# Rotating a batch of images: loads of 16 rows to a partition, with two images alternating on neighbouring partitions

## The chip, the cores and the metric

The kernel runs on one core of a Trainium2 chip. The metric is the device time of one execution in microseconds. The time before is 124.72 us, the median of 4 runs (124.68 to 124.79).

## The reference

```python
batch, c, h, w = 32, 3, 256, 256
x = np.random.randn(batch, c, h, w).astype(np.float32)

def reference(x):
    return np.rot90(x, k=-1, axes=(-2, -1)).astype(np.float32)
```

There are 96 images of 256 x 256 fp32 values, 256 KiB each, 25.17 MB in all. Each is turned by a quarter clockwise: `out[i, j] = x[255 - j, i]`. So a row of the output is a column of the input read from bottom to top. No value is changed; everything is movement.

## The kernel before

An image is cut into 32 strips of 8 rows. One strip goes to one partition (8 rows of 1 KiB, contiguous in DRAM, 8 KiB), so the 32 partitions of a quadrant hold one image and the 128 partitions hold four. This is a slab of 1 MiB, and there are 24 slabs.

For each slab, the loop at L42 does the following.

- L44: one load of 1 MiB into `t_in`, issued on the queue of SyncE (SP).
- L47 and L48 make two views. In `src` the order within a partition is column-in-group `c` (8), row `r` (8), column group `g` (32). In `dst` it is the same, but `g` now stands on the place where the partition index of the input comes out, and row and strip run backwards.
- L51: two transposes on VectorE, each for four values of `c`, 1024 elements a partition. The instruction takes the elements of a partition 32 at a time and transposes each 32 x 32 block within a quadrant: element `g` of partition `p` becomes element `p` of partition `g`. After that partition `g` holds the 8 output rows that belong to the input columns 8g to 8g+7, 8 KiB, contiguous in the output.
- L53: one store of 1 MiB from `t_out`, issued on the queue of ScalarE (ACT).

Both tiles have 12 buffers of 8 KiB a partition. A framework orders the instructions and puts in the waits: a transpose waits for its load, a store for the transposes, a load for a free buffer. It counts landings on eight semaphores, which all loads and stores use in turn; a transfer that gets a semaphore again is issued only when the transfer that had it before has landed. No order is written out by hand. PE isn't used, and GpSimd writes four constants that nothing reads.

Of the kernel before, what the change touches and what calls it, by code (L numbers as in the profile page):

```python
# [1 line left out]

# [4 lines left out]


@with_exitstack  # L10
def kernel(
    ctx: ExitStack,
    tc: tile.TileContext,
    x: bass.AP,
    out: bass.AP,
):

    nc = tc.nc
    fp32 = mybir.dt.float32

    B, C, H, W = x.shape
    P = nc.NUM_PARTITIONS
    R = 8  # L30
    G = H // R
    n_slabs = B * C * G // P
    PARTS = 2
    CP = R // PARTS

    ld_v = x.rearrange("b c h w -> (b c h) w").rearrange("(n p r) w -> n p (r w)", p=P, r=R)
    st_v = out.rearrange("b c h w -> (b c h) w").rearrange("(n p c) w -> n p (c w)", p=P, c=R)

    in_pool = ctx.enter_context(tc.tile_pool(name="in_pool", bufs=12))
    out_pool = ctx.enter_context(tc.tile_pool(name="out_pool", bufs=12))  # L40

    for n in range(n_slabs):  # L42
        t_in = in_pool.tile([P, R * W], fp32, tag="t_in")
        nc.sync.dma_start(out=t_in, in_=ld_v[n])  # L44

        t_out = out_pool.tile([P, R * W], fp32, tag="t_out")
        src = t_in.rearrange("p (r g c) -> p c r g", r=R, c=R)  # L47
        dst = t_out.rearrange("p (c g r) -> p c r g", c=R, r=R)[:, :, ::-1, ::-1]  # L48
        for k in range(PARTS):
            cs = slice(k * CP, (k + 1) * CP)  # L50
            nc.vector.transpose(out=dst[:, cs], in_=src[:, cs])  # L51

        nc.scalar.dma_start(out=st_v[n], in_=t_out)  # L53


# [1 line left out]
_INS = ['x']  # L57
_OUTS = [((32, 3, 256, 256), 'float32')]


# [23 lines left out]
```

## Time and profile before

| | us |
|---|---|
| median of 4 runs | 124.72 |
| the profiled execution, its own time | 124.71 |
| span of its instructions | 122.9 |
| VectorE busy, 48 transposes | 94.6 |
| one transpose, median | 2.040 |
| first load issued, landed | 0.73, 5.53 |
| first transpose begins | 5.55 |
| first store issued | 9.56 |
| last load issued, landed | 92.11, 111.67 |
| last store issued, landed | 115.81, 122.12 |

The time of an execution is a little longer than the span, which goes from the first instruction to the last. The profile splits the span into 40 slices and tells for each what share of it an engine was busy and how many GB/s the 16 DMA engines moved. A queue is named by a number: q1 carries the loads, q10 the stores. A DMA's packet is a piece that one DMA engine moves; every DMA also sends one small packet from each engine, which counts on the semaphore. "SPq" and "ACTq" are the sequencers that issue the DMAs. A row of a group of instructions gives the busy time and the mean of one in ns, and then how long the engine stood idle before them and what ended this.

### The profile page before, as it was taken

To read this page: it belongs to the slowest core of one execution; us is meant where nothing else is said; L and a number is where in the kernel's file an instruction comes from. 1 tells how busy PE (TensorE), PEld (TensorE's weight loads), DVE (VectorE), ACT (ScalarE), POOL (GpSimd) and SP (SyncE) were. 2 spreads that over 40 slices of the span, in tenths; PEclk is the share of its full clock that TensorE was granted. 3 is DMA by queue.
4 is the path that set the end of the run, shared out by engine and by line. 5 is a ranking of instruction groups with operands and counts; after the bars stand their busy time and mean duration, and the time that the engine had idled before them with its cause. 6 is when DMAs were issued, how large, how long until landed. Compare 5 with 4: busy or idle time off the path is not lost.

```text
span 122.9 us, 186 instructions
## 1 busy us (share of the span) xinstructions
DVE 94.6 (77%) x48; POOL 0.2 (0%) x4
## 2 busy tenths in 40 slices
DVE  0199999999797697886977969779769788696600
POOL 0000000000000000000000000000000000000000
DMA  3999999999999999999999999999999999999993
GB/s 96 424 427 381 363 427 427 427 429 429 427 427 427 427 427 427 429 429 427 427 429 427 427 427 427 429 429 429 427 429 429 427 427 429 427 427 427 427 427 160
DMA packets 6913, 50.34 MB, mean 410 GB/s; under 512 B 768, under 2 KB 768, under 8 KB 768
## 3 DMA queue, kind: packets, MB, share of 16 engines
q1 hardware_dynamic: 3456, 25.17, 49.4%
q10 hardware_dynamic: 3456, 25.17, 48.5%
q14 instruction: 1, 0.01, 0.0%
HBM read 25.17 MB, written 25.17 MB: 409 GB/s over the span
## 4 chain that ended last, share of the span: by engine, by line
DMA 79%; DVE 11%; DVEq 2%; SPq 1%; issue 0%
DMA t_in<-in_x_dram 41%; DMA out_dram<-t_out 38%; DVE t_out L51 11%; DVEq L79 2%; SPq L44 1%
## 5 line engine op out<-in xcount | busy, mean ns | idle before, releaser
L51 DVE STREAM_TRANSPOSE t_out<-t_in 128x1024 f32<-128x1024 f32 x48 | 94.6, 2054 | 21.2 <-DMA t_in<-in_x_dram 10.0
L68 POOL MEMSET const-uint8-127<- 128x1 uint8 x1 | 0.1, 102 | 0.0
L68 POOL MEMSET const-bfloat16-1.0<- 128x1 bf16 x1 | 0.1, 101 | 0.0
L68 POOL MEMSET const-float32-0.0<- 128x1 f32 x1 | 0.1, 98 | 0.2 <-issue 0.2
L68 POOL MEMSET const-float32-1.0<- 128x1 f32 x1 | 0.1, 98 | 0.0
## 6 DMA issues: line engine op xcount, KB each, us to landing
t_in<-in_x_dram SPq DMA_DIRECT2D x24, 1024.0 KB, 19.6
out_dram<-t_out ACTq DMA_DIRECT2D x24, 1024.0 KB, 16.3
```

Source lines behind the costliest of these rows:

```text
L44: nc.sync.dma_start(out=t_in, in_=ld_v[n])
L51: nc.vector.transpose(out=dst[:, cs], in_=src[:, cs])
L68: nc = _bacc.Bacc("TRN2", target_bir_lowering=False, num_devices=1)
L79: with _tile.TileContext(nc) as tc:
```

## The change

A partition now takes 16 rows (16 KiB) of an image, so an image takes 16 partitions, and a quadrant of 32 partitions holds two images. They alternate: partition `2k + i` of a quadrant has strip `k` of image `i`. A slab is 8 images, 2 MiB, and there are 12 slabs. The load is still one DMA over 128 partitions; its source is a view of three dims, 64 strips x 2 groups of images x 4096 elements, and its rows are 16 KiB long.

A transpose now handles one of the 8 values of `c`, 512 elements a partition (16 rows by 32 column groups), and its 32 outputs to a partition are 16 strips of each of two images. They go alternately to the two halves of `t_out`, which lie 8 KiB apart, one half for each image. So there are 8 transposes to a slab, 96 in all. The output keeps its strips of 8 rows: each half is stored by a DMA of its own of 1 MiB with 8 KiB to a partition, two to a slab and 24 in all. Both tiles have 6 buffers of 16 KiB a partition, the same space as before.

```diff
-    R = 8
-    G = H // R
-    n_slabs = B * C * G // P
-    PARTS = 2
-    CP = R // PARTS
+    RI, RO = 16, 8
+    K, G = H // RI, H // RO
+    I = 2
+    Q = P // (K * I)
+    n_slabs = B * C // (Q * I)
 
-    ld_v = x.rearrange("b c h w -> (b c h) w").rearrange("(n p r) w -> n p (r w)", p=P, r=R)
-    st_v = out.rearrange("b c h w -> (b c h) w").rearrange("(n p c) w -> n p (c w)", p=P, c=R)
+    ld_v = x.rearrange("b c h w -> (b c h) w").rearrange(
+        "(n i m r) w -> n i m (r w)", i=I, m=Q * K, r=RI)
+    st_v = out.rearrange("b c h w -> (b c h) w").rearrange(
+        "(n i p c) w -> n i p (c w)", i=I, p=P, c=RO)
 
-    in_pool = ctx.enter_context(tc.tile_pool(name="in_pool", bufs=12))
-    out_pool = ctx.enter_context(tc.tile_pool(name="out_pool", bufs=12))
+    in_pool = ctx.enter_context(tc.tile_pool(name="in_pool", bufs=6))
+    out_pool = ctx.enter_context(tc.tile_pool(name="out_pool", bufs=6))
 
     for n in range(n_slabs):
-        t_in = in_pool.tile([P, R * W], fp32, tag="t_in")
-        nc.sync.dma_start(out=t_in, in_=ld_v[n])
+        t_in = in_pool.tile([P, RI * W], fp32, tag="t_in")
+        nc.sync.dma_start(out=t_in, in_=ld_v[n].transpose([1, 0, 2]))
 
-        t_out = out_pool.tile([P, R * W], fp32, tag="t_out")
-        src = t_in.rearrange("p (r g c) -> p c r g", r=R, c=R)
-        dst = t_out.rearrange("p (c g r) -> p c r g", c=R, r=R)[:, :, ::-1, ::-1]
-        for k in range(PARTS):
-            cs = slice(k * CP, (k + 1) * CP)
-            nc.vector.transpose(out=dst[:, cs], in_=src[:, cs])
+        t_out = out_pool.tile([P, I, RO * W], fp32, tag="t_out")
+        src = t_in.rearrange("p (r g c) -> p c r g", r=RI, c=RO)
+        dst = t_out.rearrange("p i (c k r) -> p c r k i", c=RO, r=RI)[:, :, ::-1, ::-1, :]
+        for c in range(RO):
+            nc.vector.transpose(out=dst[:, c], in_=src[:, c])
 
-        nc.scalar.dma_start(out=st_v[n], in_=t_out)
+        for i in range(I):
+            nc.scalar.dma_start(out=st_v[n, i], in_=t_out[:, i])
```

## The prediction

> **What bounds the kernel now.** I read the overview of the page first (engines, slices, queues), then the chain of waits, then the queue's own waits, then the timeline of VectorE, and last windows of 1 us at the start, at the dip that the slices show, and at the end.
>
> ```profile
> span 122.9 us, 186 instructions
> DVE 94.6 (77%) x48; POOL 0.2 (0%) x4
> GB/s 96 424 427 381 363 427 427 427 429 429 427 427 427 427 427 427 429 429 427 427 429 427 427 427 427 429 429 429 427 429 429 427 427 429 427 427 427 427 427 160
> q1 hardware_dynamic: 3456, 25.17, 49.4%
> q10 hardware_dynamic: 3456, 25.17, 48.5%
> DMA 79%; DVE 11%; DVEq 2%; SPq 1%; issue 0%
> ...
> t_in<-in_x_dram SPq DMA_DIRECT2D x24, 1024.0 KB, 19.6
> out_dram<-t_out ACTq DMA_DIRECT2D x24, 1024.0 KB, 16.3
> ```
>
> The bytes per slice are flat at 427 to 429 GB/s from the second slice to the last but one, with one dip (381, 363). The two queues together are busy for 97.9% of 16 engines' span, VectorE for 77%, and 79% of the chain that ended last is transfers. The DMA engines are the bound. What is hard to move is 25.17 MB in and 25.17 MB out: 50.33 MB / 0.4275 MB/us = 117.7 us.
>
> ```profile
> 1.00:2.00 1.00, 0.00 (x0) 0.00 (x0) 1.00 0.45 66
> 2.00:3.00 1.00, 0.00 (x0) 0.00 (x0) 1.00 0.61 221
> 3.00:4.00 1.00, 0.00 (x0) 0.00 (x0) 1.00 0.95 401
> ...
> 11.00:12.00 1.00, 1.00 (x2) 0.00 (x0) 1.00 0.96 303
> 12.00:13.00 1.00, 1.00 (x1) 0.00 (x0) 1.00 1.04 328
> 13.00:14.00 1.00, 1.00 (x2) 0.00 (x0) 1.00 0.95 320
> ...
> 120.00:121.00 1.00, 0.00 (x0) 0.00 (x0) 1.00 0.89 377
> 121.00:122.00 1.00, 0.00 (x0) 0.00 (x0) 1.00 0.16 66
> ```
>
> The last two columns are the DMA share and the GB/s. The rest of the span is here. Start: 0 to 4 us moved 0+66+221+401 = 688 KB where 1710 were possible, a loss of 2.4 us. Dip, just as the first stores join the loads: 951 KB in 3 us where 1282 were possible, 0.8 us. End: 443 KB in the last 2.9 us where 1253 were possible, 1.9 us (landing of the last store and the closing waits). 117.7 + 2.4 + 0.8 + 1.9 = 122.8 against the span of 122.9. The profiled execution took 124.71 us, 1.8 us of it outside the span, and the median is 124.72, so a change of the span is taken as a change of the median.
>
> ```profile
> SPq L44 <- DMA t_in<-in_x_dram: 82.0, 19, 4.7
> DVE t_out L51 <- DMA t_in<-in_x_dram: 10.0, 6, 5.5
> 5.55 26.86 DVE L51 STREAM_TRANSPOSE t_out<-t_in 128x1024 f32<-128x1024 f32 x14 [5.55 <-DMA t_in<-in_x_dram]
> 33.20 3.99 DVE L51 STREAM_TRANSPOSE t_out<-t_in 128x1024 f32<-128x1024 f32 x2 [0.78 <-DMA t_in<-in_x_dram]
> ```
>
> The landing records show eight semaphores in rotation over all 48 transfers; the sixth and every later load waits until the load that had its semaphore before has landed, so about four loads (4 MB) are in flight, and the DMA engines never lack one. VectorE runs without a gap up to 32 us and then has 4.0 us of work for each 4.9 us (2 x 1.05 MB / 0.4275), in which one slab goes in and one out. It waits; nothing waits for it but the first store and the last.
>
> **The change, part by part.**
>
> (1) Load packets. 24 loads of 128 packets of 8 KB plus 16 completion packets (24 x 144 = 3456, the q1 line) become 12 loads of 128 packets of 16 KB plus 16: 1728. Stores stay at 24 with 3456. Gone are 1536 data packets and 192 completions, that is 96 and 12 on each engine. A completion packet takes 9 ns in the packet records, so 12 x 9 ns = 0.1 us. What a data packet costs beside its bytes the trace doesn't show: an 8 KB packet has 309 ns in the records, and at 427.5 GB/s one leaves each engine every 306.6 ns, so packets overlap a little. From below it is nothing (a gain of 0.1 us with the completions); from above the 9 ns of a packet of 4 bytes, 96 x 9 = 0.9 us (1.0 us in all). I take a third, 3 ns: 0.3 + 0.1 = 0.4 us gained, nearer to nothing, since records that overlap speak for small gaps.
>
> The Trainium skill (DMA: Bandwidth & Descriptors, "Why small descriptors are slow") gives about 3 cycles of overhead a packet; at the 850 MHz it names for the fabric that is an estimate of 3.5 ns, by which the gain would be 96 x 3.5 + 108 = 0.44 us. [...]
>
> (2) The loads' source now has three dims (64 x 2 x 4096), two images 1 MB apart alternating on neighbouring partitions, the destination still 128 partitions. No row has such a source. If the same 16 engines share it evenly, it costs nothing; I take that, as 64 and 128 both divide by 16, and whole rows of 16 KB are contiguous. If the engines got in each other's way, loads would go at less than 427 GB/s; that is under the rivals.
>
> (3) VectorE: 48 transposes of 1024 elements become 96 of 512, the same 49,152 elements a partition. Back to back, 14 take 26.86 us: (26.86 - 2.04) / 13 = 1.91 us from start to start, 2.04 us for one. Half of 1.91 is 0.955, the lower end if nothing is fixed. If the 0.13 us by which one is longer than the pitch is a fixed cost of each, it is (1.91 + 0.13) / 2 = 1.02. What is not in any row is the new write: neighbouring elements alternate between two places 8 KB apart, with 64 B steps instead of 32 B. From below, a write spread over two places might even be quicker, which would be worth nothing under the transfers; from above, an instruction doesn't get shorter at all (1.91). I take 1.0 us, by the nearest row: 96 us in all, for a slab of 2 MB 8.0 us against 9.8 us of transfers. It is hidden by the DMA's 117.7 us. The cover ends where first landing + 96 pitches + the end fill the span: 8.0 + 96p + 7.7 = 122.9, so p = 1.12 us (7.7 = two stores 4.9, issue, first packet and landing 2.0, closing 0.8).
>
> For that the Trainium skill (VectorE: DVE Perf Modes, "The TRN2 errata") speaks against the change: a fixed cost for every instruction, about 58 cycles, hence few large instructions. By its figure, an estimate, VectorE gets 48 x 60 ns = 2.9 us more work, all of it under the transfers.
>
> (4) Start. The first load of 2 MB lands 2.45 us later (1.05 MB / 0.4275): 5.5 becomes 8.0. Eight transposes make the first store issue at about 16.1 instead of 9.56. This costs nothing while loads fill the DMA: in 13 us they move 5.6 MB, and the eight semaphores let four or five loads of 2.1 MB go before one must wait for a store. The dip of 0.8 us when stores join moves to about 18 us; I leave its size, between 0 and twice as much (packets twice as long), as unknown: 124.7 minus or plus 0.8.
>
> (5) End. Before, the last load's packets end at 111.0 and the stores' at 121.65: 10.6 us of stores, 4.55 MB, are still to go, which is the lead that the loads got before the first store. The first store moves by 6.5 us, so the lead grows by 6.5 x 0.4275 = 2.8 to 7.35 MB. The last slab needs 0.7 (landing) + 8.1 (transposes) + about 2 (issue to first packet) = 10.8 us after the last load packet; the other 7.35 - 2.1 = 5.25 MB of stores keep the DMA busy for 12.3 us. So 1.5 us of cover is left, no bubble. The very last stores are 1 MB as before: end 1.9 us unchanged.
>
> (6) Queues. A slab now issues one load and two stores, so the rotation of eight makes a load wait for a store of the slab four or five before it, not for a load. With five, loads may lead by about 9 MB, with four by 6.9 MB; the lead is 7.35, so at worst it is cut by 0.45 MB, and 0.4 of the 1.5 us of cover at the end is left: nothing. Behind a waiting load on SP stand only loads; behind a store on ACT only stores. Buffers: six of 2 MB hold the same 12 MB.
>
> Sum: 122.9 - 0.4 = 122.5 us of span, and 124.72 - 0.4 = **124.3 us**.
>
> **The rivals.**
>
> (A) Forecast: DMA-bound as now, packets 0.1 to 1.0 us cheaper: 123.7 to 124.6, likeliest 124.3. Chance 0.55: 0.38 faster, 0.17 within the noise.
>
> (B) The rate doesn't depend on packet length at all, or the longer dip eats the gain. For it: 427 GB/s whether loads run alone or beside stores. Against it: half the completions do go. 124.5 to 124.9, about 124.7. Chance 0.15 (0.01 faster, 0.11 same, 0.03 slower).
>
> (C) VectorE becomes the bound, through the scattered write of alternating 8 KB steps. For it: even now an element takes 1.86 ns, and nothing says that the write isn't what sets this. Against: all accesses are strided already. It decides from a pitch of 1.12 us, 12% over my value; at 1.15 the span is 8.0 + 110.4 + 7.7 = 126.1 (127.9 us), at 1.25 it is 135.7 (137.5 us). Chance 0.15, all slower.
>
> (D) A bubble: loads with two images share the engines unevenly, or the semaphore wait on a store holds a load back, or transposes eat the cover of 1.5 us at the end. For it: slabs twice as coarse make every wait twice as long. Against: 4 to 5 MB of stores stand ready. 1 to 3 us: 125.5 to 127.5. Chance 0.15 (0.01 same, 0.14 slower).
>
> **How the numbers follow.** A measurement of this kernel (124.68 to 124.79) tells about 0.2%, 0.25 us, from no change. Faster 0.38 + 0.01 = 0.39; same 0.17 + 0.11 + 0.01 = 0.29; slower 0.03 + 0.15 + 0.14 = 0.32. The time is that of (A), 124.3, whose own range is 123.7 to 124.6. To leave out no more than 2 in 10 the range takes in (B), (D) and the foot of (C): 123.7 to 128.
>
> **What would show it.** Right: load queue 1728 packets; GB/s flat at 427 to 431 from 4 us on; transposes of 512 near 1.0 us apart, with gaps of over 1 us after each eight once the first third is done; first store near 16 us; last load packets near 105 us and no slice under 420 after that until the last. Wrong: transposes over 1.12 us apart and running without a gap to the end (C); slices under 400 in the middle or between the last load and the last store (D); the sum of the start, dip and end losses more than 5.5 us (B).

## The result and the profile after

The changed kernel takes 124.75 us in the median of 53 runs, before 124.72 us in 73. The ratio is 1.0033 with a 95% interval of 1.0020 to 1.0045, so it is 0.2 to 0.5% slower, although the medians are nearly equal. The reason is in the spread: before lies between 124.58 and 125.19; the changed kernel has 30 of its 53 runs from 124.43 to 124.81 (the lower group), three at 125.0, and 20 from 125.43 to 126.65 (the upper group). The profiled execution is one of the three (125.0 us); no run of the lower group left a profile.

First the overview of the changed kernel.

```profile
span 123.2 us, 199 instructions
DVE 96.6 (78%) x96; POOL 0.2 (0%) x4
GB/s 122 388 415 431 442 442 306 404 420 439 450 407 434 420 439 442 407 439 436 402 426 449 418 426 457 396 426 434 447 423 428 428 418 428 428 428 426 426 434 117
q1 hardware_dynamic: 1728, 25.17, 48.7%
q10 hardware_dynamic: 3456, 25.17, 48.3%
DMA 54%; DVE 32%; DVEq 1%; issue 1%; SPq 0%
t_in<-in_x_dram SPq DMA_DIRECT2D x12, 2048.0 KB, 12.9
out_dram<-t_out ACTq DMA_DIRECT2D x24, 1024.0 KB, 19.2
```

The load queue has its 1728 packets, and the two queues need 97.0% of 16 engines' span (97.9% before): the packets did get cheaper. The bytes per slice still stand near 427 throughout. (They scatter more, since a 16 KB packet is counted in the slice in which it starts.) A load of twice the size lands 12.9 us after its issue in the median, where the smaller one took 19.6. That is the first sign of something not foreseen: loads now hurry ahead of stores.

The waits of the queue, the waits of VectorE, and its timeline:

```profile
SPq L46 <- DMA out_dram<-t_out: 74.0, 7, 19.9
SPq L46 <- DMA t_in<-in_x_dram: 5.3, 1, 5.3
DVE t_out L52 <- DMA t_in<-in_x_dram: 12.5, 3, 8.6
8.60 64.27 DVE L52 STREAM_TRANSPOSE t_out<-t_in 128x512 f32<-128x512 f32 x64 [8.60 <-DMA t_in<-in_x_dram]
```

64 transposes take 64.27 us, a pitch of 1.0 us as forecast. The gaps after each eight that the forecast expected from the first third on aren't there: until 73 us slabs come in as fast as VectorE works. And seven of the twelve loads wait for the landing of a store, 74 us together; before, all waited for loads.

The packet records give a second reading. Take the time that has passed less (bytes moved / 428.3 GB/s): this is the mean loss of the 16 engines in us at that time. Beside it: when no load packet was on any engine for over 2 us after 28 us ("dry"); how long packets ran beyond their usual 309 or 611 ns after 28 us, summed over the engines ("stretched", in engine-us); and the time between the first and the last of the 16 landings of the last store. The last column is that execution's own time. These are sums over packet and landing records, one execution of each kernel.

| kernel | loss at 4 | at 18 | at 28 | at 120 | loads dry, us | stretched | last landings | time |
|---|---|---|---|---|---|---|---|---|
| before | 2.50 | 3.41 | 3.43 | 3.64 | none | 0.7 | 0.94 | 124.71 |
| changed | 2.77 | 2.81 | 3.63 | 3.64 | 40.9-45.4, 60.3-64.7, 80.0-84.5 | 2.0 | 1.23 | 125.00 |
| changed, again | 3.07 | 2.98 | 3.48 | 3.71 | 40.3-45.2, 61.6-66.2, 81.3-85.8 | 5.7 | 2.15 | 125.88 |
| contiguous | 2.85 | 2.77 | 3.12 | 3.63 | 39.9-43.9, 60.6-64.8, 81.0-84.2 | 10.1 | 2.46 | 125.92 |
| one store | 2.97 | 2.90 | 3.55 | 3.44 | none | 1.4 | 1.07 | 124.55 |
| load in halves | 3.01 | 3.08 | 3.72 | 3.95 | none | 0.6 | 0.90 | 125.17 |
| small start | 2.60 | 3.12 | 3.13 | 2.96 | none | 0.8 | 1.03 | 124.24 |

Read the first two rows from the left. The start costs 0.3 us more, and the first stores 0.8 as before, only later. From 28 to 120 us before loses 0.21 us more and the changed kernel none: that is most of the gain of the long packets. At 120 us both stand at 3.64. The third row has nearly the same mean at 120 and yet ends 0.9 us later, because its engines don't end together. The time is set by the slowest of 16 engines.

### The profile page after: what moved, and what is told of

Its sections match the earlier page's. It is cut to its first block, busy times and chain, and to the rows that moved or that the text cites. A ratio compares the mean times of both kernels' runs of the same rounds, so it can differ in the third digit from the quotient of the medians.

```text
span 123.2 us, 199 instructions
## 1 busy us (share of the span) xinstructions
DVE 96.6 (78%) x96; POOL 0.2 (0%) x4
## 3 DMA queue, kind: packets, MB, share of 16 engines
q1 hardware_dynamic: 1728, 25.17, 48.7%
## 4 chain that ended last, share of the span: by engine, by line
DMA 54%; DVE 32%; DVEq 1%; issue 1%; SPq 0%
DVE t_out L52 32%; DMA out_dram<-t_out 31%; DMA t_in<-in_x_dram 23%; DVEq L81 1%; DVEq L52 0%; SPq L46 0%
## 5 line engine op out<-in xcount | busy, mean ns | idle before, releaser
L52 DVE STREAM_TRANSPOSE t_out<-t_in 128x512 f32<-128x512 f32 x96 | 96.6, 1094 | 12.5 <-DMA t_in<-in_x_dram 12.5
## 6 DMA issues: line engine op xcount, KB each, us to landing
t_in<-in_x_dram SPq DMA_DIRECT2D x12, 2048.0 KB, 12.9
```

What stands on the lines that cost most here:

```text
L52: nc.vector.transpose(out=dst[:, c], in_=src[:, c])
```

## The experiments

**The changed kernel again.** No edit.

> The changed kernel again, for a second profile. Its 53 times so far fall in two groups, 30 from 124.4 to 124.8 and 20 from 125.4 to 126.7 us. Theory S (the source of two images 1 MB apart disturbs some executions), theory Q (a load that waits for a store's landing is sometimes late), theory K (slabs of 2 MB, whatever the packets) and theory L (packets of 16 KB share the engines badly with packets of 8 KB) all expect the two groups again, about 4 of 10 runs over 125.3. A profile that falls in the upper group should lose its 1 to 2 us in one place: at the start or in the dip (L, S), spread over the middle (S), or in a bubble beside a late load (Q).

Measured: 125.86 us median of 6 (124.77 to 126.75, five of them over 125.6), ratio 1.0072 (1.0044 to 1.0100). The profile fell in the upper group. Its end in windows of 1 us (the last columns are the DMA share and GB/s); before moved its last bytes at 66 GB/s from 121 to 122 and none after that:

```profile
120.00:121.00 1.00, 0.00 (x0) 0.00 (x0) 1.00 0.91 385
121.00:122.00 1.00, 0.00 (x0) 0.00 (x0) 1.00 0.18 74
122.00:123.00 1.00, 0.00 (x0) 0.00 (x0) 1.00 0.04 16
```

A share of 0.04 from 122 to 123 is less than one engine of 16 at work, while 15 are done. So the loss isn't at the start, in the dip, or spread over all engines: a straggler is 1.5 us behind the median landing (121.56, 123.11). Stretched packets stand at 45 to 48, 51, 59, 68, 86 to 92 and 97 to 100 us, most of them soon after the load queue had run dry and started again.

Do they make the straggler? The records don't name the engine, but nearly every packet begins 3 or 4 ns before another ends, so they can be joined into 16 chains (all but some 2 to 4%). The chain that ends last, at 122.78 us, has 1.55 engine-us of stretched packets, four of its seven from 45 to 48 us; the other 15 end by 121.88 with at most 0.93 each. In the contiguous kernel of the next run the four chains that end last (121.99 to 122.82) have 1.3 to 1.9 each, the other twelve at most 0.7. So in both traces the engines that end last are those with the most stretched packets.

**A contiguous source.**

```diff
-        "(n i m r) w -> n i m (r w)", i=I, m=Q * K, r=RI)
+        "(n m r) w -> n m (r w)", m=P, r=RI)
-        nc.sync.dma_start(out=t_in, in_=ld_v[n].transpose([1, 0, 2]))
+        nc.sync.dma_start(out=t_in, in_=ld_v[n])
```

> The load's source is one contiguous run of 2 MB, 16 KB to a partition, images not alternating; transposes and stores unchanged, so the images come out in scrambled places, with the same bytes and the same work. Theory S: the upper group is gone, all runs 124.4 to 124.8. Theories Q, K and L: as the changed kernel, about 4 of 10 runs over 125.3.

Measured: 126.25 us median of 4 (125.92 to 126.40), ratio 1.0125 (1.0111 to 1.0140). The alternating images aren't the cause: without them all four runs are in the upper group. Theory S falls. Why it is always there with this source and in four of ten runs with the other wasn't found.

**One store for each slab.**

```diff
-        for i in range(I):
-            nc.scalar.dma_start(out=st_v[n, i], in_=t_out[:, i])
+        nc.scalar.dma_start(out=st_v[n].transpose([1, 0, 2]), in_=t_out)
```

> One store of 2 MB for each slab in place of two of 1 MB, so that loads and stores alternate in the rotation of eight semaphores and a load waits for a load again. Theory Q: the upper group is gone, all runs 124.4 to 124.8. Theories S, K and L: about 4 of 10 runs still over 125.3.

Measured: 124.48 us median of 11 (124.41 to 124.55), ratio 0.9979 (0.9971 to 0.9988). The upper group is gone, and the kernel is a little faster than before. Its waits of the queue and its issue rows:

```profile
SPq L46 <- DMA t_in<-in_x_dram: 47.0, 7, 9.3
SPq L46 <- DVE t_out L52: 2.1, 3, 1.3
...
t_in<-in_x_dram SPq DMA_DIRECT2D x12, 2048.0 KB, 29.5
out_dram<-t_out ACTq DMA_DIRECT2D x12, 2048.0 KB, 24.5
```

Loads wait for loads again, several are in flight (29.5 us to landing), and none runs dry.

**Slabs of 2 MB with 8 KB packets.** The layout of before, two of its slabs in one load.

```diff
-    ld_v = x...rearrange("(n p r) w -> n p (r w)", p=P, r=R)
+    ld_v = x...rearrange("(n i p r) w -> n i p (r w)", i=2, p=P, r=R)
-        nc.sync.dma_start(out=t_in, in_=ld_v[n])
+        nc.sync.dma_start(out=t_in, in_=ld_v[n].transpose([1, 0, 2]))
```

> The layout and the transposes of before (8 rows, 8 KB packets, 1024 elements), but slabs of 2 MB: one load of 256 packets of 8 KB, two stores, six buffers. Theory K or Q: two groups, about 4 of 10 runs over 125.3. Theories S and L: one group, and the packet term of the forecast makes it no faster than before: 124.6 to 125.0.

Measured: 124.79 us median of 11 (124.47 to 124.88), ratio 1.0001 (0.9992 to 1.0009). Its loads wait for stores too:

```profile
SPq L45 <- DMA out_dram<-t_out: 71.4, 7, 13.6
```

Yet it has one group, no dry spell over 0.2 us, and its last landings lie within 0.47 us. So neither the slab of 2 MB nor the wait for a store is enough (K falls, Q in its plain form too); the long packet is left as what else it takes, and the next two runs test it. The packet records tell what it does. From 47 to 58 us the changed kernel moves 286 GB/s in and 145 out, 1.97 to 1; before, from 30 to 60, it is 213.6 to 213.8. That fits engines that take a packet from each queue in turn, where a load packet is now twice as long; in the chains of the changed kernel nine of ten neighbours from 47 to 58 us belong to different queues. This is theory R of the next runs.

**Contiguous source, load packets of 8 KB.** `max_dma_last_dim=8192` added to the load of the contiguous kernel.

> As the kernel with the contiguous source (images scrambled, same bytes), but its loads cut into packets of 8 KB, 256 to a load; slabs, transposes, stores and the rotation of semaphores unchanged. Theory R: packets of 16 KB and 8 KB take turns on each engine, so loads get two thirds, outrun the semaphores that they wait for, the load queue runs dry about three times for 4 us, and each restart stretches packets on a few engines, which then end 1 to 2 us after the others. With 8 KB on both sides the shares are equal, the queue doesn't run dry for more than 0.3 us, the last store's 16 landings lie within 1.0 us, and the time is 124.5 to 124.9. Rival theory P (the rotation with store waits or the contiguous source costs by itself, whatever the packets): 125.9 to 126.4 as before it.

Measured: 124.86 us median of 11 (124.77 to 125.02), ratio 1.0011 (1.0002 to 1.0020). Packet length alone takes 126.25 to 124.86: shares 1.06 to 1, no dry spell, last landings within 0.95 us. The waits for stores are still there; in the contiguous kernel with 16 KB packets and in this one they are

```profile
SPq L46 <- DMA out_dram<-t_out: 76.8, 7, 19.6
SPq L46 <- DMA out_dram<-t_out: 76.0, 7, 17.9
```

As R said, against P.

**Contiguous source, one store for each slab.** The contiguous source and the single store together, 16 KB packets.

> The contiguous source with 16 KB packets (images scrambled), but one store of 2 MB for each slab, so that no load waits for a store. Theory R: loads still get two thirds, but the load queue never runs dry in the middle; 124.2 to 124.6. Rival theory H (reading 16 KB rows of one contiguous 2 MB run is slow or uneven by itself): 125.9 to 126.4, with landings of the last store over 2 us apart.

Measured: 124.21 us median of 6 (124.15 to 124.55), ratio 0.9967 (0.9955 to 0.9978). One store in place of two, and the rotation that changes with it, takes 126.25 to 124.21. As R said, against H.

**One store, three load buffers.** `in_pool` from 6 to 3 buffers in the kernel with one store.

> One store of 2 MB for each slab as in the run that stayed at 124.4 to 124.6, and three buffers for the loads in place of six, so that a load now waits for the transposes of the third slab before it; no load waits for a store. Theory R (a dry load queue and its restart cost, whatever it waited for): the queue runs dry at most slabs, the landings of the last store spread to over 1.5 us, 125.3 to 127. Rival theory Q (it is the wait on a store's landing that costs): 124.4 to 124.6 still.

Measured: 125.86 us median of 4 (125.75 to 125.99), ratio 1.0093 (1.0079 to 1.0107). The time is as R expected, but not for R's reason. Its windows around the first store (DVE busy, POOL, clock, DMA share, GB/s):

```profile
17.00:18.00 1.00, 1.00 (x2) 0.00 (x0) 1.00 0.56 229
18.00:19.00 1.00, 1.00 (x2) 0.00 (x0) 1.00 1.15 377
19.00:20.00 1.00, 1.00 (x2) 0.00 (x0) 1.00 0.98 205
20.00:21.00 1.00, 1.00 (x2) 0.00 (x0) 1.00 1.01 336
21.00:22.00 1.00, 1.00 (x2) 0.00 (x0) 1.00 1.13 344
22.00:23.00 1.00, 1.00 (x2) 0.00 (x0) 1.00 0.81 295
```

With three buffers the first three loads end at 18 us just as the first store comes, and this dip costs 2.2 us of all engines instead of 0.8. After that the load queue is dry eight times for 0.1 to 0.9 us, and none of these costs anything; the last landings lie within 0.94 us. This run can't speak for R.

**A small start.** One store for each slab, the first 8 images as two slabs of the kernel before, and five large buffers on each side in place of six.

```diff
+    for n in range(I):
+        s_in = small_in.tile([P, RO * W], fp32, tag="s_in")
+        nc.sync.dma_start(out=s_in, in_=ld_s[n])
...
+        nc.scalar.dma_start(out=st_v[0, n], in_=s_out)
-    for n in range(n_slabs):
+    for n in range(1, n_slabs):
```

> One store for each slab of 2 MB, and the first 8 images as two slabs of the kernel before (1 MB, 8 KB packets, two transposes of 1024). Theory R with the start as a separate loss (the first packets of the three-dim load begin at 2.1 us where those of before begin at 1.7): loss at 4 us falls from about 2.9 to 2.5 us, no dry queue, 124.0 to 124.3. If the start loss has nothing to do with the form of the first load: 124.4 to 124.6.

> The kernel with a small start again, for the interval: 124.0 to 124.3 by theory R, with no load dry for over 0.5 us.

Measured: 124.18 us median of 5 (124.08 to 124.29), ratio 0.9957 (0.9943 to 0.9970), and in a second set of runs 124.14 of 5 (124.10 to 124.18), ratio 0.9957 (0.9945 to 0.9968). The loss at 4 us is 2.60 where the kernel with 2 MB from the start has 2.97. The form of the first load isn't all that counts: every kernel that begins with 2 MB loses 2.76 to 3.07, the contiguous and the 8 KB ones too. Nor is its size: the last kernel below begins with 1 MB from the source of three dims and loses 3.01. Only the load of before, plain and of 1 MB, loses 2.50 to 2.60. This version beats both kernels, by 0.5 us.

**Loads run dry for want of buffers.** One store; four buffers for the first four slabs, two for the other eight.

> One store for each slab of 2 MB (no load waits for a store); the buffers of the loads are divided, four for the first four slabs and two for the other eight, so that from the seventh slab on a load waits for the transposes of the slab two before it. The start is as with six buffers. Loads should run dry once for about 11 us (from about 40) and then about five times for 2 to 3 us, while stores keep the DMA engines busy. Theory R (a load queue that was dry for several us and starts again stretches packets on some engines): stretched packets 2 to 6 us after each such restart, 1 or more engine-us each, the landings of the last store over 1.5 us apart in most executions, 125 to 127. Rival theory Q (only waits on a store's landing on all 16 engines do this): no stretched packets after 28 us, 124.4 to 124.7.

Measured: 128.16 us median of 6 (127.45 to 130.50), ratio 1.0269 (1.0242 to 1.0295). In windows of 2 us:

```profile
90.00:92.00 2.00, 2.00 (x3) 0.00 (x0) 1.00 1.15 430
92.00:94.00 2.00, 2.00 (x3) 0.00 (x0) 1.00 0.92 307
94.00:96.00 2.00, 2.00 (x3) 0.00 (x0) 1.00 0.88 324
...
116.00:118.00 2.00, 2.00 (x4) 0.00 (x0) 1.00 0.61 254
118.00:120.00 2.00, 1.11 (x2) 0.00 (x0) 1.00 0.00 0
```

The load queue was dry at 39 to 53, 68 to 72 and 89 to 92 us. The first restart stretched nothing, the second 0.7 engine-us, the third 15 (91 to 96 us: the DMA share stays near 0.9 and the bytes fall). That one had waited for transposes, not for a landing, so a wait for a landing isn't needed. Another 2.5 us went into a bubble near 119 in which the last slab was late and no queue had work, so the time can't be laid to restarts alone, and the landings, all delayed by the bubble, don't show the spread expected.

**Two dry spells, nothing else.** One store, five load buffers and one that slabs 4, 7 and 10 share.

> One store for each slab of 2 MB as in the run that stayed at 124.4 to 124.6; five buffers for the loads and one shared by slabs 4, 7 and 10, so that load 7 waits for the transposes of slab 4 (until about 49) and load 10 for those of slab 7 (until about 73). The load queue should be dry twice for 3 to 9 us and stores should fill the DMA engines all the while; no load waits for a store. Theory R (restart after several dry us stretches packets, not each time): stretched packets of 0 to 15 engine-us within 6 us of each restart, the landings of the last store over 1.2 us apart, times spread from 124.5 to 126.5 with a median over 124.8. If a restart costs nothing: 124.4 to 124.6 and no stretched packets after 28 us beyond the single one of 0.5 us.

Measured: 124.51 us median of 11 (124.38 to 124.69, and one of 125.27), ratio 0.9991 (0.9980 to 1.0003). The load queue was dry from 46.8 to 52.8 us and for 1.2 us at 76. No packet was stretched behind either, the single one of 0.5 us at 65 us aside. A dry spell of 6 us can cost nothing: R in this form was wrong.

**One dry spell with 8 KB packets.** Before, with 11 load buffers and one that slabs 11 and 12 share.

> The kernel before, with 11 buffers for the loads and one shared by slabs 11 and 12, so that load 12 waits for the transposes of slab 11. The load queue is dry once, for about 6 us from about 60, and the stores that are ready (some 3 MB) fill the DMA engines. Packets are 8 KB on both sides. Theory R without a part for packet length: stretched packets of 0 to 15 engine-us behind the restart, 124.7 to 126, runs spread over more than 0.5 us. If long packets are needed for it: 124.6 to 124.9 like before, no stretched packets after 28 us.

Measured: 124.68 us median of 11 (124.56 to 124.91), ratio 1.0002 (0.9993 to 1.0011). The dry spell didn't come about (none over 0.1 us): inconclusive.

**Three stores for each slab.** The second store of the changed kernel cut into 7 rows and 1.

> The changed kernel with the second store of each slab cut into 7 rows and 1 row of a partition, three stores a slab: four transfers a slab, so that the rotation of eight lets a load wait for the load two before it and for no store. Loads keep 16 KB packets. If the rotation is the cause (the load queue runs dry for 4 us because a load waits for a store's landing): no dry spell over 2 us after 28 us, the last landings within 1.2 us, all runs within 0.5 us of each other, at 124.6 to 125.2 (1536 more store packets cost up to 0.5 us). If stores in several DMAs beside long load packets are the cause whatever the rotation: two groups again, with runs 1 to 2 us over the lowest.

Measured: 125.35 us median of 5 (125.20 to 125.42), ratio 1.0053 (1.0040 to 1.0065). One group, so several stores don't make two by themselves, as far as five runs tell (with four in ten in the upper group, five would miss it about once in 13). It is 0.15 us above the range expected. Against the expectation there is a dry spell (31.4 to 38.0): two loads still waited for stores. Stretched packets follow from 38 to 45 (2.5 engine-us), and after 85 us, with stores alone, short packets cost 0.4 us. Landings lie 1.12 us apart.

**The changed kernel, each load in two halves.** Two DMAs of 8 rows to a partition.

> The changed kernel with each load cut into two DMAs of 8 rows a partition, so 8 KB packets and 1 MB each; two stores a slab as before. Four transfers a slab. If long packets and the dry queue are the cause: shares of loads and stores equal, no dry spell over 0.5 us after 28 us, all runs 124.5 to 125.0. If the alternating source or the scattered transposes are the cause: runs up to 126 again.

Measured: 125.15 us median of 5 (125.10 to 125.34), ratio 1.0040 (1.0027 to 1.0054). One group, shares 0.99 to 1, nothing dry: the alternating source and the scattered transposes by themselves don't make runs of 126, again as far as five runs tell. The edit undoes both sides at once, the long packets and the waits for stores (17 of its 18 waits are for loads), so it doesn't part them. The level is 0.15 over what I expected. Against the kernel with one store its loss grows by 0.23 from 28 to 120 us where the other's falls by 0.11.

## Why the prediction was wrong

By its own steps:

(1) **Packets: right.** The records have 309 ns for 8 KB with the next packet 306 ns after it, and 611 for 16 KB with the next after 607: 2 x 306 - 607 = 5 ns for each packet saved, where I took 3. 96 x 5 + 12 x 9 ns = 0.6 us. The kernel with one store loses 0.34 us less from 28 to 120 than the one with 8 KB halves. The Trainium skill (DMA: Bandwidth & Descriptors, "Why small descriptors are slow") puts it at about 3 cycles, by my estimate 3.5 ns; the measured 5 ns agree in size.

(2) **The source of three dims: nearly right.** Pure loads run at 428 GB/s and more (611 ns each), evenly enough. With one store the contiguous source took 124.21 where this one took 124.48 (ratios 0.9967 and 0.9979, whose intervals overlap), so up to 0.3 us may be the price of three dims; the first packet comes at 2.10 us instead of 1.72.

(3) **VectorE: right.** A pitch of 1.0 us, and rival (C) is out: it idles 12.5 us waiting for loads, 8.6 of them before the first.

(4) **Start: wrong by 0.3 to 0.5 us.** I moved the first landing to 8.0 us (measured: 8.6) and called the rest free. The loss at 4 us is 2.5 to 2.6 with the first load of before and 2.8 to 3.1 with all others, whether they have 2 MB in the plain form (2.85, 3.04) or 1 MB in three dims (3.01). What makes it wasn't taken apart. The dip kept its size (0.8), as assumed.

(5) **End: right, with luck.** There was no bubble. But the last load packet ended at 99.4 us, not near 105, with 9.3 MB of stores still to go instead of 7.35, because loads had more than half of the engines, which the step didn't foresee. Stores filled the engines until 121.

(6) **Queues: the step that failed.** It says of the lead: "at worst it is cut by 0.45 MB", and of the cost: "nothing". It reckoned with equal shares and some 2 us from issue to first packet. Measured: loads get two bytes for each one of stores, so a load of 2 MB is through in 7.3 us where slabs take 9.8; and a load issued onto engines that are busy with stores has its first packet 4 us later (issued at 41.30, 60.84, 80.70; first packets at 45.35, 64.71, 84.54). The lead of the loads was 7.46 MB when the first store's packets began (20.7 us), as forecast (7.35); but it didn't stay there, it grew to 9.2 MB by 41 us. That is the bound of about 9 MB that the step itself gives for five slabs. (In the kernel with 2 MB slabs and 8 KB packets the lead never exceeds 6.8 MB.) So the lead ran up against the landing that a load waits for, and the queue was dry for 4.5 us three times. That stores keep the DMA busy meanwhile was right; that it costs nothing was not. The Trainium skill (DMA: Bandwidth & Descriptors, "Queues, rings and completion order") says that an engine takes turns between queues by packet. The prediction drew on that page for the overhead of a packet and not for this. The trace agrees: 1.97 to 1, as with one piece of 8 or 16 KB a turn.

What the runs show: the upper group goes when either side is undone, the packet length (126.25 to 124.86) or the second store and with it the rotation (126.25 to 124.21, and 124.75 to 124.48). Without step (6) the rest of the sum holds in part: one store gains 0.24 us, with the small start 0.5, where 0.4 were forecast. Apart from the kernels with three and with divided buffers, which lost their time elsewhere too, only those with repeated dry spells of over 3 us and 16 KB packets have runs of 126, and their engines end up to 2.5 us apart; stretched packets stand behind their restarts in 8 of 12 cases (three each in the changed kernel's two profiles, the contiguous one and the one with divided buffers; a single packet stretched by 0.5 us, which most traces have around 60 us, isn't counted). They also occur where nothing was dry (0.95 engine-us at 37 to 38 us with one store, 1.5 at 32 to 33 in the second small start), and cost nothing there. What is **open** is what a restart needs to stretch packets: one of 6 us and one of 14 us cost nothing, one of 3 us cost 15 engine-us. Rival (D) named the wait on a store, but as a bubble; it was not a bubble but an uneven end, so it is luck that most of the upper group lies in its 125.5 to 127.5. The median of 124.75 lies where rival (B) had it, by luck as well: the packets did get cheaper.

The sum as it stands: packets -0.6, start +0.3 to +0.5, ends further apart 0.1 to 1.5: between -0.2 and +1.4. Measured are -0.3 to +0.1 in the lower group and +0.7 to +1.9 in the upper, so some 0.5 us of the slowest runs, which left no profile, isn't accounted for.

## What to carry to other kernels

When two DMA queues share the engines, the longer packet gets the larger share; before lengthening the packets on one side, follow each queue by itself and ask what it waits for once it is ahead. Count the DMAs of one round against the number of landing semaphores: one more store to a slab changed what the loads wait for. And look at the landings of the slowest engine, not only at the mean GB/s; long packets paid once loads no longer waited for stores (-0.2%), and beginning with two of the old slabs paid as much again (-0.4% together).

## What had not been expected of the hardware

- A queue that starts on engines busy with another queue has its first packet 3.8 to 4.1 us after the issue (9.56 to 13.58 for the first store of before, 41.30 to 45.35 and 80.70 to 84.54 for loads), against 1.0 to 1.4 us at the very start.
- Load packets of 16 KB ran up to 1.1 us instead of 0.61 while a queue was starting in the first profile of the changed kernel, up to 1.7 in the second, and up to 2.3 in the kernel with divided buffers. Stores kept their 309 ns to within 16 ns in nearly all records, but not right behind a restart in the upper group: 21 store packets of the contiguous kernel and 5 of the changed kernel's second profile were stretched, most to 550 to 700 ns. The profile at 125.0 us has none.
- Transposes of 1024 and 512 elements have pitches of 1.91 and 1.00 us. If the scattered write costs nothing, that is 0.1 us fixed and 1.77 ns an element; no run has 512 elements with the old write, so the two aren't parted.
